# Hybrid decoder trunk on one core: the systems' products move behind the next pair's projections, and ScalarE takes copies out of PSUM

## The chip, the cores and the metric

The kernel runs on one core of one Trainium2 chip. The metric is the device time of one execution in microseconds (us). The engines of the core are TensorE (PE in the profile; PEld is its weight load), VectorE (DVE), ScalarE (ACT), GpSimd (POOL) and SyncE (SP, which issues nearly all DMAs here). PSUM is the memory that TensorE writes, SBUF the working memory.

## The reference, cut to what matters

One layer over 2048 tokens of width 1024. A combined projection `p = rms_norm(x) @ w_in` feeds five branches; each branch's output is projected up, weighted with a sigmoid gate, and the sum goes through `w_out`, a residual and a last norm. Three pieces of it concern the change:

```
# retention: rotate q and k, then chunks of 128 with a fixed decay
x1 * cos - x2 * sin,  x2 * cos + x1 * sin
scores = (q @ k.T) * seg;  y = scores @ v + (q * exp(cum)) @ prev_state
# RWKV-7: one state update per token
sa = state @ a_t
state = state * w_t + sa b_t^T + v_t k_t^T
y_t = state @ r_t
```

The kernel computes the RWKV recurrence in chunks of 64 tokens. For each head and chunk it forms a triangular system from products of decayed keys and "a" vectors, inverts it, and uses the inverse in a chain over the chunks.

## The kernel before, in words

The sequence is worked through in four blocks of 512 tokens. In each block the stages are: cross-attention (`mem`), preparation and solve for RWKV (`rwkv_first`), retention (`ret`), the RWKV chain (`rwkv`), the state-space branch, GLA, and the output product. Activations are kept transposed, 128 channels by 512 tokens to a tile.

A projection (`proj`, through `mm3`) is 24 matmuls of 128x128 by 128x512: 8 slices of the input, each in three parts, since values are split into a high and a low part. It accumulates in one of three PSUM tiles named `acc`; other products use three tiles `br` and two `y`. Weights come through a ring of four tiles `wt`, loaded by SP; in the first block they are loaded raw and split by ScalarE (`L378`) and GpSimd (`L379`). All matmuls but transposes are recorded at line L305, tensor-tensor operations of VectorE at L299, scalar-tensor-tensor ones at L302, and most activations at L296. Work tiles in SBUF are 42 tiles of one tag, `s`.

Gate and up-projection work of the previous branch waits in a queue (`self.fq`), in pieces: a gate piece is one projection, an up piece of the memory branch is 6 matmuls. `self.fill(n)` takes n pieces from it; `self.solve(n)` takes n steps from a second queue `self.dq`, which holds the 31 steps of the triangular solve.

`rwkv_prep` loops over four pairs of heads. For each pair: projection k, its squares, projection r, then `late()` of the pair before (with a piece of the queue ahead of it), the small products with `w2a2` (L1107, L1108), a chain of some twenty elementwise operations on VectorE, ScalarE and GpSimd that ends in the tiles `ars` and `kbs` (L1142 to L1146), their stores to DRAM (L1150), projection v, and then the systems' products (L1158): 32 matmuls of 64x64. Their masked result goes to `Ab` and, by four copies, to `dia` (L1165). `late` does the bonus term and the transposes of v, and stores both (L1173, L1179).

`rwkv_solve` prepares `X` and the 31 steps, each a multiplication (L1203) and a reduction (L1204) on VectorE; the later a step the larger. `ret` then runs `rope` for q and k (two projections each, four multiplications on VectorE that read both `acc` tiles from PSUM, two sums on GpSimd, eight stores at L695), `v_tok` (the values by token: 96 matmuls into four PSUM tiles, then four copies out at L714), and two pairs of heads. Each pair begins with a transposed k that VectorE scales (L764). `rwkv_sys`, which uses the solve (transposes L1219 and L1221, copies L1226), comes after `ret`.

Outside the very first stage a scheduler orders the instructions of each engine when the program is built, by its own estimate of their durations; the order in the program is the priority. On the chip every engine, and SP's queue of DMAs, runs through its list in that order.

Of the kernel before, what the change touches and what calls it, by code (L numbers as in the profile page):

```python
# [13 lines left out]
ALU = mybir.AluOpType  # L14
# [3 lines left out]
P = 128  # L18
# [20 lines left out]
def _groups():  # L39
# [3 lines left out]
    def add(name, c):  # L43
        g[name] = len(cols)
        cols.append(np.asarray(c, np.int64))

    def nat(name, key, n):
        for i in range(n):
            add(f"{name}{i}", _OFF[key] + 128 * i + np.arange(128))

    half = np.concatenate([64 * h + 2 * np.arange(32) for h in range(4)])
    for nm in ("q", "k"):
        add(f"ret_{nm}A", _OFF[f"ret_{nm}"] + half)
        add(f"ret_{nm}B", _OFF[f"ret_{nm}"] + half + 1)
    nat("ret_g", "ret_g", 4)
# [89 lines left out]
class K:  # L145
# [531 lines left out]
    def rope(self, nmq, sn, cs):  # L677

        nc = self.nc
        st = [self.s() for _ in range(2)]  # L680
        A = self.proj(f"ret_{nmq}A")
        B = self.proj(f"ret_{nmq}B")
        for i in range(2):
            t1, t2, o = self.s(), self.s(), self.s()
            if i == 0:
                self.tt(t1, A, cs, ALU.mult)
                self.tt(t2, B, sn, ALU.mult)
                nc.gpsimd.tensor_tensor(o, t1, t2, ALU.subtract)
            else:
                self.tt(t1, B, cs, ALU.mult)  # L690
                self.tt(t2, A, sn, ALU.mult)
                nc.gpsimd.tensor_tensor(o, t1, t2, ALU.add)
            for h in range(4):
                r = 64 * (h % 2) + 32 * i
                nc.sync.dma_start(st[h // 2][r:r + 32, :], o[32 * h:32 * h + 32, :])  # L695
        return st

    def v_tok(self, key):

        ps = [self.ps("acc") for _ in range(3)] + [self.ps("y")]  # L700
        for k in range(KT):
            (hi, lo), = self.load_w(("wv_" + key, k), 4)
            whi, wlo = (t.rearrange("p h d -> p (h d)") for t in (hi, lo))
            xhi, xlo = self.xh[k]
            for c in range(4):
                cs_ = slice(c * P, (c + 1) * P)
                self.mm(ps[c], xhi[:, cs_], whi, start=(k == 0), stop=False)
                self.mm(ps[c], xhi[:, cs_], wlo, start=False, stop=False)
                self.mm(ps[c], xlo[:, cs_], whi, start=False, stop=(k == KT - 1))
        vs = []  # L710
        for c in range(4):
            v = self.s()
            nc_copy = (self.nc.scalar.copy, self.nc.vector.tensor_copy)[c % 2]
            nc_copy(v, ps[c])  # L714
            vs.append(v)
        return vs

# [25 lines left out]
    def ret(self, sc):  # L743
        nc = self.nc
        sn, cs = self.tables
        q = self.rope("q", sn, cs)
        self.solve(K.FILL["solve"][0])
        k = self.rope("k", sn, cs)
        self.solve(K.FILL["solve"][1])
        V = self.v_tok("ret")  # L750
        self.solve(K.FILL["solve"][2])
        res = []
        for p in range(2):
            qh = self.s()
            self.tt(qh.rearrange("p (c t) -> p c t", t=P), q[p].rearrange("p (c t) -> p c t", t=P),
                    self.c["qd"][:, p * P:(p + 1) * P].unsqueeze(1).to_broadcast([P, 4, P]), ALU.mult)
            tp = self.ps("br")
            for c in range(4):
                self.tr(tp[:, c * P:(c + 1) * P], k[p][:, c * P:(c + 1) * P])
            kt = self.s()  # L760
            for j in range(2):
                h = 2 * p + j
                v4 = lambda t: t.rearrange("p (c h d) -> p c h d", h=2, d=64)[:, :, j, :]
                nc.vector.tensor_scalar(v4(kt), v4(tp), self.c["kd"][:, h:h + 1], None, ALU.mult)  # L764

            sp = self.ps("br")
            for c in range(4):
                cs_ = slice(c * P, (c + 1) * P)
                for j in range(2):
                    self.mm(sp[64 * j:64 * j + 64, cs_], kt[:, c * P + 64 * j:c * P + 64 * j + 64],  # L770
                            V[c][:, (2 * p + j) * P:(2 * p + j + 1) * P])
            S = self.states("Sret", self.S_ret, p, 4)
            for c in range(4):
                self.stt(S[c + 1], S[c], self.c["gC"][:, p:p + 1], sp[:, c * P:(c + 1) * P], ALU.mult, ALU.add)
            pts = []
            for j, sps in enumerate(self.scores(k[p], q[p])):
                pt = self.s()
                h = 2 * p + j
                self.tt(pt.rearrange("p (c t) -> p c t", t=P), sps.rearrange("p (c t) -> p c t", t=P),
                        self.c["dec"][:, h * P:(h + 1) * P].unsqueeze(1).to_broadcast([P, 4, P]), ALU.mult)  # L780
                pts.append(pt)
            ys = [self.ps("y") for _ in range(2)]
            self.solve(K.FILL["solve"][3])
            self.fill(K.FILL["ret"][0])
            for j in range(2):
                for c in range(4):
                    cs_ = slice(c * P, (c + 1) * P)
                    self.mm(ys[j][:, cs_], V[c][:, (2 * p + j) * P:(2 * p + j + 1) * P], pts[j][:, cs_],
                            start=(c == 0), stop=False)
            self.fill(K.FILL["ret"][1])  # L790
            for c in range(4):
                cs_ = slice(c * P, (c + 1) * P)
                for j in range(2):
                    r = slice(64 * j, 64 * j + 64)
                    self.mm(ys[j][:, cs_], S[c][r, :], qh[r, cs_], start=False, stop=(c == 3))
            res += self.finish_pair(sc, "ret", p, ys, self.cv["one"], K.FILL["ret"][2])
            self.solve(K.FILL["solve"][4])
        return res
# [283 lines left out]
    def rwkv_prep(self, wa, pairs):  # L1082
        nc = self.nc
        v3 = lambda t: t.rearrange("p (c t) -> p c t", t=64)
        am = self.c["am"]
        Ab = []
        gC = self.s((P, 4, 8), tag="gC", bufs=2)
        dia = self.s((P, 32, 32), tag="blk", bufs=3)
# [5 lines left out]
        late = None  # L1094
        for i, p in enumerate(pairs):
# [28 lines left out]
            rk = self.s()  # L1124
            self.stt(rk, r, self.p["r_k"][:, pc], kp, ALU.mult, ALU.mult)
            rk = self.parts(rk, self.pick(7))
# [3 lines left out]
            v = self.s()  # L1130
# [6 lines left out]
            ars, kbs = [], []  # L1137
# [13 lines left out]
                                      t.rearrange("p c a t -> p c (a t)"))  # L1151
            v = self.shift(8 + p)

            ap = self.ps("br")
            for c in range(8):
                for q in range(2):
                    rq = slice(64 * q, 64 * q + 64)
                    self.mm(ap[rq, c * 64:c * 64 + 64], kbs[c // 4][rq, c % 4, 1, :], ars[c // 4][rq, c % 4, 0, :])  # L1158
            ab = self.s((P, 8, 64))
            self.tt(ab, ap.rearrange("p (j t) -> p j t", t=64),  # L1160
                    am[:, 0:64].unsqueeze(1).to_broadcast([P, 8, 64]), ALU.mult)
            Ab.append(ab)
            for g in range(4):
                rg, b = slice(32 * g, 32 * g + 32), g % 2
                (nc.scalar.copy, nc.gpsimd.tensor_copy)[g % 2](  # L1165
                    dia[rg, :, i * 8:i * 8 + 8], ab[rg, :, 32 * b:32 * b + 32].rearrange("s j t -> s t j"))

            def late(p=p, rk=rk, v=v):
                bps = self.ps("br")
                self.msum(bps, self.bones_r, rk)  # L1170
                bv = self.s()
                self.tt(bv, bps, v, ALU.mult)
                nc.sync.dma_start(self.bvd[p], bv)  # L1173
                tp = self.ps("br")
                for c in range(4):
                    self.tr(tp[:, c * P:(c + 1) * P], v[:, c * P:(c + 1) * P])
                vt = self.s()
                nc.scalar.copy(vt, tp)
                nc.sync.dma_start(self.vtd[:, p, :].rearrange("(c r) d -> r c d", r=P),  # L1179
                                  vt.rearrange("p (c d) -> p c d", d=P))  # L1180

        self.fill(K.FILL["late"][3])
        late()
        return Ab, dia, gC

    def rwkv_solve(self, dia):

# [25 lines left out]
    def rwkv_sys(self, Ab, X):  # L1213

        nc = self.nc
        self.solve()
        self.fill(K.FILL["sys"][0])
        xa = self.s((P, 32, 32), tag="blk", bufs=3)
        nc.vector.transpose(xa, X.rearrange("p s c -> p c s"))  # L1219
# [3 lines left out]
        for i in range(4):  # L1223
            for g in range(4):
                r, b = slice(32 * g, 32 * g + 32), g % 2
# [131 lines left out]
    def rwkv_first(self, sc):  # L1357

        wa = self.shift(12)
        self.nc.scalar.activation(wa[0:64, :], wa[0:64, :], AF.Tanh)  # L1360
        Ab, dia, gC = self.rwkv_prep(wa, range(4))
        X, self.dq = self.rwkv_solve(dia)
        return Ab, X, gC

    def rwkv(self, sc):
# [300 lines left out]
```

## Time and profile before

| | us |
|---|---|
| median of 3 runs (3663.86 to 3673.31) | 3667.82 |
| the profiled execution, its own time | 3665.22 |
| its span, first to last instruction | 3663.4 |
| TensorE busy | 3444.2 |
| VectorE busy | 1992.8 |
| ScalarE busy | 983.5 |
| GpSimd busy | 917.4 |

The mean granted clock of TensorE is 0.966 of full. An idle time is given with what released it: `<-POOL s L1145` means that the engine waited for a GpSimd instruction of line 1145 that writes a tile `s`. A timeline merges like instructions; `x16` counts them.

### The profile page before, as it was taken

How to read it: one execution, taken by the hardware profiler on the slowest of the kernel's cores; microseconds unless marked ns; L12 is line 12 of the kernel's file. 1: busy time of each engine (PE TensorE's matmuls, PEld its weight loads, DVE VectorE, ACT ScalarE, POOL GpSimd, SP SyncE). 2: the span in 40 equal slices, each digit the busy share in tenths (PEclk: the TensorE clock that was granted, in tenths of full speed). 3: DMA queues.
4: the chain of work that ended last, by engine and by line, in shares of the span. 5: the costliest groups of instructions: out<-in, count | busy, mean ns of one | idle time of the engine just before them, and what ended most of it. 6: DMA issues, size and time to landing. Idle time of an engine off the chain costs nothing. (4 is left out here: it accounts for less than half of the span.)

```text
span 3663.4 us, 51984 instructions
## 1 busy us (share of the span) xinstructions
PE 3444.2 (94%) x20368; PEld 2766.4 (76%) x20368; DVE 1992.8 (54%) x3188; ACT 983.5 (27%) x1797; POOL 917.4 (25%) x919
## 2 busy tenths in 40 slices
PE   7878999998999899999999899999999989999998
PEld 6667777777777677888877677788887768778887
DVE  6685456635467645552356854554346664554243
ACT  5423224342442111312133121222123311131212
POOL 3655335555423110211103210021101311020110
PEclk9889899999999999999999999999999999999999
DMA  6566646676765444545565554445465645344555
GB/s 213 191 204 208 212 166 220 210 256 225 268 207 187 157 156 140 190 155 170 174 213 194 178 157 153 156 151 188 156 220 187 191 155 165 132 163 150 172 170 192
DMA packets 269541, 673.17 MB, mean 184 GB/s; under 512 B 27232, under 2 KB 81008, under 8 KB 269296
## 3 DMA queue, kind: packets, MB, share of 16 engines
q1 hardware_dynamic: 268864, 669.32, 54.8%
q8 instruction: 161, 2.64, 0.3%
q14 instruction: 84, 0.69, 0.1%
q10 hardware_dynamic: 432, 0.52, 0.0%
HBM read 503.54 MB, written 162.00 MB: 182 GB/s over the span
## 5 line engine op out<-in xcount | busy, mean ns | idle before, releaser
L305 PE MATMUL acc<-xhi,wt 128*128 128x512 f32 x5632 | 1832.3, 401 | 21.3 <-ACT s L296 9.5
L305 PEld LDWEIGHTS acc<-xhi,wt 128*128 128x128 f32 x5632 | 1076.6, 192 | 264.4 <-issue 13.3
L305 PE MATMUL acc<-xlo,wt 128*128 128x512 f32 x2816 | 1124.9, 399 | 2.5 <-DVE xlo L1542 1.8
L305 PE MATMUL acc<-s,wt 128*128 128x512 f32 (+1 forms) x2448 | 602.4, 396 | 30.5 <-ACT s L714 15.7
L305 PEld LDWEIGHTS acc<-xlo,wt 128*128 128x128 f32 x2816 | 541.7, 192 | 118.1 <-DVE xlo L1542 3.0
L305 PEld LDWEIGHTS acc<-s,wt 128*128 128x128 f32 x2448 | 459.0, 192 | 131.6 <-ACT s L714 17.0
L302 DVE SCALAR_TENSOR_TENSOR s<-s,acc 128x512 f32<-128x512 f32 x192 | 131.5, 685 | 668.5 <-PE acc L305 363.3
L379 POOL TENSOR_TENSOR wt<-wr,wt 128x512 fp32r<-128x512 f32 (+1 forms) x256 | 354.1, 1389 | 379.7 <-ACT wt L378 360.2
L302 DVE SCALAR_TENSOR_TENSOR s<-s,s 128x512 f32<-128x512 f32 (+1 forms) x458 | 368.1, 807 | 31.9 <-ACT s L296 19.8
L379 POOL TENSOR_TENSOR s<-s,s 128x512 fp32r<-128x512 f32 x120 | 159.9, 1341 | 858.7 <-ACT s L378 650.4
L296 ACT ACTIVATE s<-acc 128x512 f32<-128x512 f32 x232 | 136.4, 596 | 646.1 <-PE acc L305 633.5
L305 PE MATMUL br<-s,s 64*64 64x64 f32 (+6 forms) x2432 | 213.4, 284 | 75.0 <-POOL s L1145 33.6
L305 PEld LDWEIGHTS br<-s,s 64*64 64x64 f32 (+3 forms) x2432 | 164.7, 171 | 128.0 <-POOL s L1145 38.3
L378 ACT CAST wt<-wr 128x512 fp32r<-128x512 f32 (+1 forms) x256 | 155.4, 611 | 293.2 <-PE acc L305 102.5
L1406 POOL TENSOR_TENSOR mg<-mg,s 128x512 f32<-128x512 f32 x64 | 87.2, 1363 | 545.9 <-DVE s L302 545.9
L378 ACT CAST s<-s 128x512 fp32r<-128x512 f32 x182 | 112.7, 620 | 344.6 <-DVE s L302 328.2
L296 ACT ACTIVATE s<-s 128x512 f32<-128x512 f32 (+1 forms) x204 | 119.3, 611 | 287.2 <-DVE s L299 116.6
L299 DVE TENSOR_TENSOR s<-s 128x512 f32<-128x512 f32 (+1 forms) x167 | 162.4, 977 | 5.8
L305 PE MATMUL acc<-wt,xhi 128*128 128x512 f32 x384 | 123.2, 401 | 26.6 <-DMA wt<-kw 10.0
L305 PE MATMUL y<-s,s 128*64 128x64 f32 (+4 forms) x2112 | 136.8, 253 | 6.9 <-DVE s L299 4.4
L305 PEld LDWEIGHTS y<-s,s 128*64 128x64 f32 (+2 forms) x2112 | 112.2, 151 | 37.8 <-DVE s L299 10.9
L299 DVE TENSOR_TENSOR s<-s,s 128x512 f32<-128x512 f32 (+2 forms) x154 | 119.1, 798 | 37.6 <-ACT s L296 36.0
(218 smaller groups left out, 3208.7 us busy)
## 6 DMA issues: line engine op xcount, KB each, us to landing
wt<-kw SPq DMA_DIRECT2D x712, 512.0 KB, 3.3
kw<-wt SPq DMA_DIRECT2D x240, 512.0 KB, 3.1
wr<-in_wg_dram SPq DMA_DIRECT2D x176, 256.0 KB, 3.8
s<-in_xT_dram SPq DMA_DIRECT2D x88, 256.0 KB, 5.0
ard<-s SPq DMA_DIRECT2D x32, 256.0 KB, 2.2
kbd<-s SPq DMA_DIRECT2D x32, 256.0 KB, 2.5
s<-kbd SPq DMA_DIRECT2D x32, 256.0 KB, 4.1
s<-ard SPq DMA_DIRECT2D x32, 256.0 KB, 4.8
```

The lines of the kernel that those rows point to most:

```text
L296: self.nc.scalar.activation(out, in_, f, bias=bias, scale=scale, **kw)
L299: self.nc.vector.tensor_tensor(out, a, b, op)
L302: self.nc.vector.scalar_tensor_tensor(out, a, s, b, op0, op1)
L305: i = self.nc.tensor.matmul(out, lhsT=lhsT, rhs=rhs, start=start, stop=stop)
L378: self.nc.scalar.copy(hi, src)
L379: (eng or self.nc.gpsimd).tensor_tensor(lo, src, hi.bitcast(F32), ALU.subtract)
L1406: (eng or self.pick({"ret": 0, "rwkv": 1, "ssd": 2, "gla": 3}[key])).tensor_tensor(merged[d], merged[d], t, ALU.add)
```

## The change

In `rope`, the two projections A and B are each copied by ScalarE from PSUM to a work tile; the multiplications read the copies. In `v_tok`, all four copies of retention's values are ScalarE's; for GLA they still alternate between ScalarE and VectorE. In `rwkv_prep`, the systems' products with their mask and copies move into `late`, which runs after the next pair's projections k and r. The last pair's `late`, the queue piece ahead of it and the setting up of the solve leave `rwkv_first`: they run after the rotation of q in `ret`, as the first entry of the solve's queue.

```diff
     def rope(self, nmq, sn, cs):
...
-        A = self.proj(f"ret_{nmq}A")
-        B = self.proj(f"ret_{nmq}B")
+        A, B = self.s(), self.s()
+        for t, c in ((A, "A"), (B, "B")):
+            nc.scalar.copy(t, self.proj(f"ret_{nmq}{c}"))
...
     def v_tok(self, key):
...
-            nc_copy = (self.nc.scalar.copy, self.nc.vector.tensor_copy)[c % 2]
-            nc_copy(v, ps[c])
+            if c % 2 and key != "ret":
+                self.nc.vector.tensor_copy(v, ps[c])
+            else:
+                self.nc.scalar.copy(v, ps[c])
...
     def ret(self, sc):
         q = self.rope("q", sn, cs)
+        self.fill(K.FILL["late"][3])
         self.solve(K.FILL["solve"][0])
...
     def rwkv_prep(self, wa, pairs):
...
             v = self.shift(8 + p)
-            ap = self.ps("br")
-            for c in range(8):
-                for q in range(2):
-                    rq = slice(64 * q, 64 * q + 64)
-                    self.mm(ap[rq, c * 64:c * 64 + 64], kbs[c // 4][rq, c % 4, 1, :], ars[c // 4][rq, c % 4, 0, :])
-            ab = self.s((P, 8, 64))
...
-            def late(p=p, rk=rk, v=v):
+            def late(i=i, p=p, rk=rk, v=v, ars=ars, kbs=kbs):
+
+                ap = self.ps("br")
+                for c in range(8):
+                    for q in range(2):
+                        rq = slice(64 * q, 64 * q + 64)
+                        self.mm(ap[rq, c * 64:c * 64 + 64], kbs[c // 4][rq, c % 4, 1, :], ars[c // 4][rq, c % 4, 0, :])
+                ab = self.s((P, 8, 64))
...
                 bps = self.ps("br")
                 self.msum(bps, self.bones_r, rk)
...
-        self.fill(K.FILL["late"][3])
-        late()
-        return Ab, dia, gC
+        return Ab, dia, gC, late
...
     def rwkv_sys(self, Ab, X):
         self.solve()
+        X, = X
...
     def rwkv_first(self, sc):
...
-        Ab, dia, gC = self.rwkv_prep(wa, range(4))
-        X, self.dq = self.rwkv_solve(dia)
+        Ab, dia, gC, late = self.rwkv_prep(wa, range(4))
+        X = []
+
+        def begin():
+            late()
+            x, self.dq = self.rwkv_solve(dia)
+            X.append(x)
+
+        self.dq = [begin]
         return Ab, X, gC
```

## Rows read from the trace of the kernel before

**Rows 1.** The page, part 1: busy us (share) x instructions of each engine.

```profile
PE 3444.2 (94%) x20368; PEld 2766.4 (76%) x20368; DVE 1992.8 (54%) x3188; ACT 983.5 (27%) x1797; POOL 917.4 (25%) x919
```

**Rows 2.** Waits of TensorE, whole span: us in total, times, longest us.

```profile
PE br L305 <- POOL s L1145: 33.6, 12, 4.6
PE br L305 <- DVE s L302: 22.0, 4, 6.1
...
PE acc L305 <- DVE s L299: 16.0, 7, 4.6
PE acc L305 <- ACT s L714: 15.7, 3, 5.7
PE acc L305 <- DMA wt<-kw: 10.0, 7, 2.3
```

**Rows 3.** Waits of TensorE from 220 to 345 us, the first block's retention.

```profile
PE acc L305 <- POOL wt L379: 8.3, 3, 4.8
```

**Rows 4.** Timeline of TensorE, fourth block: start us, us, what, idle before.

```profile
2879.27 1.54 PE L305 MATMUL br<-s,w2a 64*128 64x256 f32 x8
...
2894.02 0.61 PE L305 MATMUL acc<-xhi,wt 128*128 128x512 f32 x2
2897.06 0.68 PE L305 MATMUL br<-s,s 64*64 64x64 f32 x16 [2.43 <-POOL s L1145]
...
2899.31 1.22 PE L305 MATMUL acc<-xhi,wt 128*128 128x512 f32 x2
...
2923.57 0.68 PE L305 MATMUL br<-s,s 64*64 64x64 f32 x16 [2.56 <-POOL s L1145]
```

**Rows 5.** Windows: 16 stretches at half clock; us, PE busy, PEclk, DMA.

```profile
2898.10:2901.50 3.40, 3.32 (x22) 0.50 0.85 224
...
sum 78.60, PE 69.85; mean PE 4.37
```

**Rows 6.** Timeline of VectorE, fourth block, retention with the solve.

```profile
2927.63 1.25 DVE L1191 STREAM_TRANSPOSE blk<-blk 128x1024 f32<-128x1024 f32 x1 [0.66 <-POOL blk L1165]
...
2938.55 0.68 DVE L299 TENSOR_TENSOR s<-acc,s 128x512 f32<-128x512 f32 x1
...
2945.36 0.68 DVE L299 TENSOR_TENSOR s<-acc,s 128x512 f32<-128x512 f32 x1
...
2952.19 0.68 DVE L299 TENSOR_TENSOR s<-acc,s 128x512 f32<-128x512 f32 x1
...
2978.66 1.21 DVE L1221 STREAM_TRANSPOSE blk<-blk 128x1024 f32<-128x1024 f32 x1
2979.78 0.66 DVE L714 COPY s<-acc 128x512 f32<-128x512 f32 x1
...
2981.88 0.86 DVE L764 TENSOR_SCALAR s<-br,cst 128x256 f32<-128x256 f32 x2
```

**Rows 7.** Timeline of TensorE, fourth block, after V's matmuls.

```profile
2983.76 2.93 PE L305 MATMUL acc<-s,wt 128*128 128x512 f32 x6 [5.71 <-ACT s L714]
```

**Rows 8.** Timeline of ScalarE, the same stretch.

```profile
2978.77 4.46 ACT L1226 COPY s<-blk 32x256 f32<-32x256 f32 x7 [50.65 <-DVE blk L1219]
```

**Rows 9.** Timeline of SP's queue, fourth block: start us, us, issue.

```profile
2922.64 0.37 SPq L1150 DMA_DIRECT2D ard<-s  x1
...
2955.12 2.41 SPq L695 DMA_DIRECT2D s<-s  x4
```

**Rows 10.** Groups by line and form: busy us, mean ns | idle before.

```profile
L296 ACT ACTIVATE s<-acc 128x512 f32<-128x512 f32 x232 | 136.4, 596 | 646.1 <-PE acc L305 633.5 <-issue 12.6
L299 DVE TENSOR_TENSOR s<-s,s 128x512 f32<-128x512 f32 x116 | 98.0, 870 | 37.6 <-ACT s L296 36.0
L299 DVE TENSOR_TENSOR s<-acc,s 128x512 f32<-128x512 f32 x48 | 31.4, 682 | 19.1 <-PE acc L305 19.1
```

**Rows 11.** Chain that ended last, 3000 to 3020 us: start us, us, what.

```profile
3005.31 11.11 PE acc L305 x48
```

**Rows 12.** The page, part 6: DMA issues, KB each, us to landing.

```profile
wt<-kw SPq DMA_DIRECT2D x712, 512.0 KB, 3.3
```

More of the change, by code (lines that the diff above doesn't have):

```diff
@@ L1152, in rwkv_prep @@
             v = self.shift(8 + p)
-            ap = self.ps("br")
-            for c in range(8):
-                for q in range(2):
-                    rq = slice(64 * q, 64 * q + 64)
-                    self.mm(ap[rq, c * 64:c * 64 + 64], kbs[c // 4][rq, c % 4, 1, :], ars[c // 4][rq, c % 4, 0, :])
-            ab = self.s((P, 8, 64))
[L1160 to L1166, printed above, removed]
-            def late(p=p, rk=rk, v=v):
+            def late(i=i, p=p, rk=rk, v=v, ars=ars, kbs=kbs):
[5 more added lines that the diff above has]
+                ab = self.s((P, 8, 64))
+                self.tt(ab, ap.rearrange("p (j t) -> p j t", t=64),
+                        am[:, 0:64].unsqueeze(1).to_broadcast([P, 8, 64]), ALU.mult)
+                Ab.append(ab)
+                for g in range(4):
+                    rg, b = slice(32 * g, 32 * g + 32), g % 2
+                    (nc.scalar.copy, nc.gpsimd.tensor_copy)[g % 2](
+                        dia[rg, :, i * 8:i * 8 + 8], ab[rg, :, 32 * b:32 * b + 32].rearrange("s j t -> s t j"))
                 bps = self.ps("br")
```

## The prediction

> **What bounds the kernel now.** The page comes first. TensorE is busy for 94% of the span, no other engine for more than 54% [rows 1]. So the time is TensorE's work plus its idle time, and an edit is worth what it takes from that idle time, or from the work done at a low clock. The view of waits, for TensorE alone, then shows where the idle time lies [rows 2]. The two largest entries, 33.6 + 22.0 = 55.6 us in 16 waits, stand in front of one thing: the systems' products of rwkv_prep (L1158), four in each of the four blocks of tokens. Four further entries belong to the stretch after them, the retention stage: 16.0 us for accumulators that VectorE's rotation still reads, 15.7 us for ScalarE's copies of V, 10.0 us for weights not landed [rows 2], and in the first block 8.3 us for weights that GpSimd splits [rows 3]. That makes 50.0 us.
>
> The timeline of TensorE shows what one product wait looks like [rows 4]. The small products L1107 end at 2880.81 (2879.27 + 1.54). TensorE goes on with projections until 2894.63, then waits 2.43 us. The products start at 2897.06, 16.25 us after L1107. In between it had about 13.8 us of work, since the scheduler took the chain on VectorE and GpSimd for shorter than it is. The two projection matmuls ahead of the wait took 0.61 us, the two after it 1.22 us. The windows give the reason: after each of the 16 waits stands a stretch with granted clock 0.50, the lower of the two levels (1.2 GHz). They add up to 78.6 us, 69.85 of them busy [rows 5]. What the engine did before each was to stand idle.
>
> For the retention stage I read three engines in one stretch. VectorE runs the 62-step solve from 2927.63 to 2979.78 without a pause, and the rotation's multiplications stand between its steps [rows 6]. TensorE waits 5.71 us at 2983.76 for ScalarE's V copy [rows 7]. ScalarE had stood 50.65 us in front of L1226, which needs the end of the solve, with the V copies queued behind [rows 8].
>
> **Part 1, the products behind the next pair's projections.** Work stays the same; order changes. Two projections of 24 matmuls take 11.1 us [rows 11], 5.55 each. Between L1107 and the products TensorE will have the pair's v projection, the next pair's k and r projections, and a unit of the queue: a gate (5.55) three times of four, an up product (6 matmuls, 1.4) once, since the queue begins with gate, gate, up, gate. That is 16.65 + 5.55 = 22.2 us, or 18.0 us. The chain needs 16.25 us, so the wait goes: -55.6 us. The first block is slower, with waits near 6 us [rows 2], so its chain is some 3 us longer; there the pair with the short unit still waits. I leave +4 us for that and its clock. The half-clock time goes with the waits. It costs at most half of its busy time, 34.9 us, and at least nothing; I take 30, because projection matmuls, most of that time, took exactly double.
> The Trainium skill (TensorE: Matmul & The Clock Gate, section Terms) prices such time as throttled time times one minus the clock ratio: 39.3 us as an estimate from that page, by which the sum would be 9 us lower. The trace bears the halving out, but 8.75 us of the stretch were idle.
>
> The four stores of a pair (ard, kbd) keep their place on SP's queue, as do bvd and vtd of the first three pairs; the last pair's follow q's eight stores, whose inputs are ready before the solve starts. Nothing waits for them before the chain stage.
>
> **Part 2, the last pair and the solve behind the rotation of q.** The order is now v, q's two projections, a gate, the products: 22.2 us after L1107 instead of 16.25. The solve starts 4.06 us after the products' start, as now (2923.57 to 2927.63) [rows 4, 6]. What is queued behind the solve on VectorE is the rotation of k and retention's first pair.
>
> **Part 3, ScalarE's copies.** 16 copies of A and B and 8 of V at 0.596 us [rows 10] are 14.3 us on an engine busy for 27%, hidden in its 50.65 us pause [rows 8] and its like; if that cover went, 3.6 us a block. An accumulator is then free 0.6 us after its last matmul instead of after VectorE's turn, so 16.0 us go, and 15.7 us go if the V copies stand ahead of L1226. They should: now the solve's last transpose (2978.66) and the first V copy (2979.78) are neighbours [rows 6], so any later start of the solve turns their order round. SP's stores of the rotated k hold the weight loads up [rows 9]; they wait for GpSimd and so for VectorE. With the solve started later VectorE is less far behind at that point, and I let the 10.0 go, and the 8.3 of the first block, where ScalarE's weight casts stood behind L1226 too. In all -50.0 us. Six or seven of those waits were long, and after one the six matmuls took 2.93 us instead of 1.4 [rows 7, 11]: another -9.
> 32 multiplications now read two SBUF tiles: 0.870 us instead of 0.682 on the mean [rows 10]. Sixteen, those of k, fall into the solve. The Trainium skill (GPSIMD Engine Reference, 1. Specifications) says that GpSimd shares its SBUF interface with VectorE and contends with instructions that have two SBUF inputs; that speaks against this edit, the two rows agree with it, and by it the sum would be 16 x 0.19 = 3 us higher.
>
> **What is late next.** VectorE. The scheduler lined the multiplications at 2938.55, 2945.36 and 2952.19 up with the ends of successive projections [rows 6]. TensorE needs 5.55 us for each, VectorE took 6.8: it runs 1.25 times slower than the order supposes, so it falls behind as long as it is full. TensorE next needs VectorE in retention's first pair: the scaled transpose of k (L764), for which V's copies had been the cover [rows 6, 7]. In the new order the products take some 2.4 us (2897.06 to 2899.31 and a little), k's rotation 11.1 and V's 96 matmuls 22.2: V ends 35.7 us after the products' start, 31.7 after the solve's. VectorE needs 31.7 x 1.25 = 39.6 us for what stands before L764. So a new wait of 8 us a block, 32 us, and 1.7 us of clock each, 7 us: +39. Bounds: nothing, if other work stands in front of it; and 17.7 us a block if L764 follows the whole solve. The solve without eight multiplications is 52.15 - 5.4 = 46.7 us, with four 49.4; it ends 53.4 us after the products' start, 17.7 after V.
>
> **Sum.** The profiled execution took 3665.2 us. 3665.2 - 55.6 - 30 + 4 - 50 - 9 + 39 = 3563.6. The median of the runs is 2.6 us above that execution: **3566 us**.
>
> **Rivals.**
> No late VectorE (12%): the queue's units cover L764. For it: a gate is 5.55 us and one is queued there. Against it: the order supposes no wait, so it has no reason to put more than a short unit in front. -39: 3527 us.
> ScalarE stays behind the solve (16%): L1226 is still queued ahead of V's copies, now all four on that engine. Then TensorE waits from V's end to the end of the solve and its copies, 17.7 + 4.46 = 22.2 us a block [rows 8]; 89 in place of 32: 3623 us. Against it: the solve starts later.
> The change doesn't do what it says (6%): the scheduler goes by readiness, and puts the products where they stand now if weights or accumulators of the next projections aren't free. Then -55.6, -30 and +4 stay out: 3648 us. Against it: TensorE ran into k's projection ahead of the products already now [rows 4].
> Slower (6%): the weight ring. TensorE no longer rests while SP stands in front of the ard and kbd stores [rows 9]. A load lands 3.3 us after its issue [rows 12] and its slot is due three tiles, 8.2 us, later, which leaves 4.9. The stores come about as much later than the order supposes as the products do now, 2.4 us, so this is hidden. The rival decides if loads land 10 us after issue or later: each pair then waits 6 us + 1.9 of clock, 16 x 7.9 = 126 us: 3692 us.
>
> **How the numbers follow.** The forecast has 55%, with a range of its own from 3545 to 3590. With two of the rivals, 3527 and 3623, the range from 3525 to 3625 holds 83%. 5% are left for mixtures that end near 3668. A measurement of this kernel tells no change from 0.3%, 11 us. Faster: 55 + 12 + 16 + 6, less 1 for scatter: 0.88; same 0.05; slower 0.07.
>
> **What would show it.** Right: the entries GpSimd L1145 and VectorE L302 ahead of 64x64 products are gone; no half clock between pairs; products stand 18 to 22 us after L1107; ScalarE's V copies stand ahead of L1226; TensorE waits some 8 us a block for L764. Wrong: the products still wait; V copies behind L1226; waits for weights in rwkv_prep. The prediction fails most easily in the new order of retention's first pair, which the trace of before doesn't show.

## The result, and the profile after

The changed kernel takes 3613.65 us (median of 4 runs, 3611.5 to 3618.59) against 3665.84 us (4 runs): a ratio of 0.9858, 95% interval 0.9837 to 0.9879. It is faster by 52 us; forecast were some 100. 3613.65 lies inside the stated range, 3525 to 3625, but outside the forecast's own, 3545 to 3590. The profiled execution has a span of 3616.7 us, 46.7 less than before; its mean granted clock is 0.967. Of the 46.7 us, 15.6 are busy time of TensorE (3444.2 before [rows 1]) and 31.1 idle time:

```profile
PE 3428.6 (95%) x20368; PEld 2760.3 (76%) x20368; DVE 1993.1 (55%) x3180; ACT 997.8 (28%) x1821; POOL 914.8 (25%) x919
```

The view of waits, TensorE alone, whole span (engine, what it waited for: us in total, times, longest):

```profile
PE br L305 <- DVE s L768: 26.9, 5, 6.2
PE br L305 <- DVE s L299: 25.0, 12, 5.5
PE acc L305 <- ACT wt L378: 11.5, 3, 7.2
...
PE acc L305 <- DMA wt<-kw: 9.2, 6, 2.4
...
PE acc L305 <- POOL wt L379: 7.5, 5, 4.2
...
PE br L305 <- POOL s L1149: 6.3, 2, 3.1
```

Gone are the waits for GpSimd (L1145, now L1149) and VectorE in front of the systems' products, all but 6.3 us and 1.4 in the first block, and those for the rotation and for V's copies [rows 2]. The 6.3 us stand at the first pair of blocks 3 and 4. There 14 of the 32 products stand ahead of one of the four projections that were to cover them, and the chain was not done; in the fourth block:

```profile
2804.08 1.08 PE L305 MATMUL br<-s,s 64*64 64x64 f32 x14 [3.14 <-POOL s L1149]
```

To weigh the first two lines, these are the same entries before (L764 is now L768):

```profile
PE acc L305 <- POOL wt L379: 8.9, 4, 4.8
PE acc L305 <- ACT wt L378: 7.0, 1, 7.0
PE br L305 <- DVE s L299: 6.7, 8, 4.1
PE br L305 <- DVE s L764: 4.7, 2, 4.3
```

So two waits grew where large ones went: for a VectorE result of L299 by 18.3 us, and for the scaled transpose of k by 22.2.

**The first of them** stands in the preparation. TensorE in the fourth block, around the products of the second pair and of the third (start us, us; x32 counts instructions; in brackets the idle time in front and what ended it):

```profile
2839.06 1.15 PE L305 MATMUL br<-s,s 64*64 64x64 f32 x32
...
2841.24 1.54 PE L305 MATMUL br<-s,w2a 64*128 64x256 f32 x8
...
2859.82 1.52 PE L305 MATMUL acc<-s,wt 128*128 128x512 f32 x6
2861.28 1.15 PE L305 MATMUL br<-s,s 64*64 64x64 f32 x32
...
2866.46 1.73 PE L305 MATMUL br<-s,w2a 64*128 64x256 f32 x8 [2.93 <-DVE s L299]
```

The systems' products (64x64) start without a wait, 18.5 us after the end of the small products of their pair (2842.78 to 2861.28; before, 16.25 for this pair). But the next small products (`w2a`) now wait 2.93 us. VectorE at that time:

```profile
2864.45 0.75 DVE L302 SCALAR_TENSOR_TENSOR s<-u,par,s 128x512 f32<-128x512 f32 x1 [2.58 <-ACT s L296]
2865.12 0.68 DVE L302 SCALAR_TENSOR_TENSOR mg<-s,acc 128x512 f32<-128x512 f32 x1
2865.72 0.69 DVE L299 TENSOR_TENSOR s<-br,cst 128x512 f32<-128x512 f32 x1
```

The mask multiplication `s<-br,cst`, which reads the systems' products and so frees their `br` tile, ends at 2866.41, and the small products start at 2866.46. There are three `br` tiles; `late` now takes all three (products, bonus, transposes), and the small products follow it. The mask stands behind the shift of the next r, whose projection was issued just before the 6 matmuls of an up product. VectorE was itself idle for 2.58 us in front of that shift, until ScalarE had handed it over, while the products had ended at 2862.43; whether the mask, put ahead of the shift in VectorE's list, would take the wait away was not tried. Where a whole gate was the piece (2839.06) the wait is absent, but for 3.39 us in block 1 and 0.85 in block 2. Over the four blocks the waits for the mask are 18.5 us, 14.3 of them behind the short piece.

**The second** stands in retention's first pair. TensorE, VectorE and ScalarE in the fourth block:

```profile
2931.54 1.64 PE L305 MATMUL acc<-s,wt 128*128 128x512 f32 x6
...
2939.84 5.31 PE L305 MATMUL br<-s,s 128*64 128x128 f32 x32 [6.20 <-DVE s L768]
```
```profile
2935.98 1.68 DVE L299 TENSOR_TENSOR blk<-blk,blk 128x900 f32<-128x900 f32 x1
2937.70 1.09 DVE L1206 TENSOR_REDUCE blk<-blk 128x30 f32<-128x900 f32 x1
...
2939.30 0.87 DVE L768 TENSOR_SCALAR s<-br,cst 128x256 f32<-128x256 f32 x2
```
```profile
2929.39 1.90 ACT L717 COPY s<-acc 128x512 f32<-128x512 f32 x3 [22.75 <-PE acc L305]
...
2948.57 5.39 ACT L1229 COPY s<-blk 32x256 f32<-32x256 f32 x8 [16.55 <-DVE blk L1222]
```

V's copies stand ahead of the solve's copies (L1229), as forecast. VectorE goes through the solve up to its last step but one (128x900) before it comes to L768, and TensorE waits 6.20 us.

The granted clock is read from the windows. The sums over all stretches at 0.50 in the preparation (8 of them) and in retention (9, the last one shown), then the last stretch and the sum of a list for retention before (8):

```profile
sum 40.94, PE 36.09; mean PE 4.51
...
2936.50:2946.74 10.24, 6.90 (x36) 0.50 0.00 0
sum 64.84, PE 49.81; mean PE 5.53
```
```profile
2983.40:2986.81 3.41, 3.04 (x7) 0.50 0.00 0
sum 37.55, PE 32.53; mean PE 4.07
```

The list before begins with the stretch at 218.60 (6.83 us, 5.29 of them busy), which stands behind the last product wait of the first block and is among the 16 of [rows 5] too; without it retention had 30.7 us, 27.24 busy. The preparation before had, beside those 16, one stretch that stands behind no product wait (95.72, 6.83 us, 6.17 busy); its counterpart is among the 8 after. So in the preparation the half clock fell from 85.4 to 40.9 us, and in retention it rose from 30.7 to 64.8. At each first pair's wait for L768 stand 10.24 us at 0.50, in which the 32 matmuls of the states and the scores take 5.31 us; after the 5.71 us for V before it was 3.41 us [rows 7].

### The profile page after: what moved, and what is told of

Its sections match the earlier page's. It is cut to its first block, busy times and chain, and to the rows that moved or that the text cites. A ratio compares the mean times of both kernels' runs of the same rounds, so it can differ in the third digit from the quotient of the medians.

```text
span 3616.7 us, 52010 instructions
## 1 busy us (share of the span) xinstructions
PE 3428.6 (95%) x20368; PEld 2760.3 (76%) x20368; DVE 1993.1 (55%) x3180; ACT 997.8 (28%) x1821; POOL 914.8 (25%) x919
## 3 DMA queue, kind: packets, MB, share of 16 engines
q1 hardware_dynamic: 268864, 669.32, 55.6%
## 4 chain that ended last, share of the span: by engine, by line
PE 55%; DVE 10%; issue 1%; DMA 1%; ACT 1%; POOL 0%; SPq 0%; DVEq 0%; POOLq 0%; ACTq 0%
PE acc L305 44%; PE br L305 6%; PE y L305 4%; DVE s L302 4%; DVE s L299 2%; DVE blk L299 2%; DVE blk L1206 1%; PE br L317 1%; DMA s<-ard 1%; ACT s L296 1%; DVE s L339 0%; DVE s L329 0%; DMA s<-in_xT_dram 0%; ACT blk L1171 0%; DMA s<-kmd 0%
## 5 line engine op out<-in xcount | busy, mean ns | idle before, releaser
L379 POOL TENSOR_TENSOR wt<-wr,wt 128x512 fp32r<-128x512 f32 (+1 forms) x256 | 354.8, 1391 | 380.1 <-ACT wt L378 369.3
L379 POOL TENSOR_TENSOR s<-s,s 128x512 fp32r<-128x512 f32 x120 | 159.7, 1339 | 816.6 <-ACT s L378 672.3
L378 ACT CAST wt<-wr 128x512 fp32r<-128x512 f32 (+1 forms) x256 | 155.2, 611 | 268.3 <-PE acc L305 89.6
L378 ACT CAST s<-s 128x512 fp32r<-128x512 f32 x182 | 112.8, 620 | 341.4 <-DVE s L302 316.6
L299 DVE TENSOR_TENSOR s<-s,s 128x512 f32<-128x512 f32 (+2 forms) x186 | 144.2, 803 | 44.5 <-ACT s L296 42.2
L299 DVE TENSOR_TENSOR s<-s 128x512 f32<-128x512 f32 (+1 forms) x167 | 163.0, 980 | 5.8
```

Of the source, the lines that this page charges most:

```text
L299: self.nc.vector.tensor_tensor(out, a, b, op)
L378: self.nc.scalar.copy(hi, src)
L379: (eng or self.nc.gpsimd).tensor_tensor(lo, src, hi.bitcast(F32), ALU.subtract)
```

## The experiments

The theory to test: the moved products bring the gain; the shortfall is the two new waits with their clock, and waits for weights that didn't go. Rivals are named at each run.

**1. Only the copies; 2. only the moves.** The first has the hunks in `rope` and `v_tok`, the second all the others.

> The kernel before with ScalarE's copies of the rotation's operands and of all of retention's values, and nothing moved. Theory (the moved products bring the gain, and the copies give back what they take away by making VectorE's scaled transpose of k late): the 16.0 us of waits for accumulators held by the rotation go, some of the 15.7 us for V's copies too, and waits for the scaled transpose with half-clock time behind them take their place; 3665.8 before, 3645 to 3672 here, a ratio of 0.995 to 1.002. Rival (the copies bring most of the gain of 52 us, the moved products little): 3615 to 3635, a ratio below 0.992.

Measured: 3683.43 us, ratio 1.0051 (1.0037 to 1.0066), slower than before and outside both ranges. The copies alone lose 20 us. In the profile the accumulator waits for the rotation are gone, but:

```profile
PE acc L305 <- DMA wt<-kw: 20.3, 11, 2.7
PE acc L305 <- ACT s L717: 18.6, 3, 6.6
```
```profile
sum 85.37, PE 68.73; mean PE 5.73
```

Weights come later (10.0 before), V's copies still stand behind the solve's, and retention has 85.4 us at half clock instead of 37.6 (both lists with the stretch at 218): 36.2 us more busy time there, half of which, 18.1 us, would be loss. By the page, TensorE's busy time grew by 12.5 us (3444.2 to 3456.7) and the span by 17.4, so the clock is most of the difference and not all of it. The wait for L768 that I had expected did not appear.

> The changed kernel with the moved products, last pair and solve, but the rotation reads PSUM and the copies of V alternate, as before. Theory (the moved products bring the gain): the 56 us of product waits are replaced by some 27 us of others, half-clock time in the preparation falls by some 41 us of stretch, 20 us of time; the accumulator waits of the rotation stay or grow a little: 3610 to 3632, a ratio of 0.985 to 0.991. Rival (the copies bring it): 3640 to 3660, a ratio of 0.993 to 0.999.

Measured: 3616.77 us, 0.9873 (0.9853 to 0.9892). The moves bring 47 of the 52 us; the interval overlaps that of the whole change. Part of the rotation's waits stays, and waits for V's copies on VectorE stand beside them (the profiled execution took 3601.86 us, 15 less than the median):

```profile
PE acc L305 <- DVE s L299: 12.1, 4, 4.0
...
PE acc L305 <- DVE s L714: 9.0, 4, 3.5
```

**3. The transposed k scaled by ScalarE.**

```diff
-                nc.vector.tensor_scalar(v4(kt), v4(tp), self.c["kd"][:, h:h + 1], None, ALU.mult)
+                self.act(v4(kt), v4(tp), AF.Copy, scale=self.c["kd"][:, h:h + 1])
```

> The changed kernel, but ScalarE scales the transposed k instead of VectorE (L768). Theory (VectorE behind the solve, alone, makes the wait of 26.9 us and the half clock after it): the waits go, the half-clock stretches after them (four of about 10.2 us, half of it lost) too: 3613.7 less 23 to 27 of waits less about 20 of clock, 3567 to 3585. Rival (the wait only moves on to the next results of VectorE, the masked scores and the states, which stand behind the same solve): the entry of L768 is gone and others of VectorE (L299, L302) grow by as much, 3605 to 3617.

Measured: 3612.27 us, 0.9865 (0.9846 to 0.9884), no change. My theory of a single late instruction falls. TensorE, fourth block:

```profile
2937.96 2.25 PE L305 MATMUL br<-s,s 128*64 128x128 f32 x32
...
2948.46 3.62 PE L305 MATMUL y<-s,s 128*128 128x128 f32 x16 [7.13 <-DVE s L299]
```

The 32 matmuls come earlier and at full clock, and then TensorE waits 7.13 us for the masked scores, also VectorE's and behind the same solve. Waits of this kind (`y <- DVE s L299`) are 32.6 us in all, 4.9 in the changed kernel.

**4. One more piece ahead of the third pair's products.** `"late": (1, 1, 2, 1)` in place of `(1, 1, 1, 1)`.

> The changed kernel with two pieces of the queue instead of one ahead of the third pair's small products, so that a full projection follows the short up product there. Theory (the small products wait because the mask multiplication, which frees their PSUM tile, has only the short piece as cover): the waits of 18.5 us for the mask fall by the 15 or so that stand at the third pair, with some of the half clock behind them: 3592 to 3605. Rival (the tile is short wherever the piece stands, since the mask stands behind VectorE's other work, or the piece taken from later leaves a hole there): the waits move, 3608 to 3625.

Measured: 3654.32 us, 0.9969 (0.9957 to 0.9981), 41 us slower than the changed kernel, worse than either range. The wait entry of the mask fell from 25.0 to 11.8 us, as forecast, and was paid for elsewhere:

```profile
PE br L305 <- DVE s L768: 40.0, 8, 8.3
PE acc L305 <- ACT s L296: 26.0, 10, 6.2
```

All later pieces of the queue changed places, gates for up products. Run 6 holds them in place.

**5. Pieces ahead of the late product in retention.**

```diff
+            if p == 0:
+                self.fill(2)
             sp = self.ps("br")
...
-            self.fill(K.FILL["ret"][1])
+            self.fill(K.FILL["ret"][1] - 2 * (p == 0))
```

> The changed kernel, but in retention's first pair two pieces of the queue (a short one and a whole gate) stand ahead of the product that needs the scaled transpose of k (L768), and two fewer behind it; VectorE's work is the same. Theory (VectorE is late by a few us and TensorE merely lacks cover; scaling on ScalarE only moved the wait on to the masked scores): the L768 waits of 22.7 us at four first pairs go, the masked scores have the next short piece and arrive in time, the half clock behind goes: 3613.7 - 22.7 - about 20 = 3570, 3565 to 3590. Rival (VectorE's solve is the bound of the whole stretch, so a wait of the same size comes up further back, at the masked scores, the states or the systems' stage): 3605 to 3620.

Measured: 3608.34 us, 0.9845 (0.9826 to 0.9865). The rival is right but for a few us: L768 falls to 8.3 us, and 23.2 us stand at the masked scores.

```profile
PE y L305 <- DVE s L299: 23.2, 16, 4.8
```

Runs 3 and 5 say the same: not one instruction is late, all that VectorE does behind the solve is.

**6. The same pieces in the same order, the short one earlier.** `"late": (1, 2, 1, 0)`.

> The changed kernel with the same pieces of the queue in the same order, but a gate follows the short up product already ahead of the second pair, and none is left for the last pair; behind the preparation the queue stands as before. Theory (the third pair's small products wait for the mask because their only cover is the short piece; with one piece more in all, the loss came from the shifted queue in retention): the waits for the mask at the third pair go (some 15 us with block 1's), those of L768 stay within 3 us of 26.9, the last pair's products may wait 1 us a block: 3590 to 3606. Rival (the mask's tile is short wherever pieces stand): 3610 to 3620.

Measured: 3602.28 us, 0.9821 (0.9804 to 0.9838), 11 us under the changed kernel. The mask's entry falls from 25.0 to 9.8 us, L768 stays at 25.8. So the short piece as only cover made most of that wait (block 1's 3.39 us stays), and with the queue held in place run 4's loss is gone. That the shift made the loss is argued from this, not shown.

**7. The small products ahead of the systems' products.** `late()` stands behind the two `w2a2` loops instead of before them.

> The changed kernel with the small products of the next pair ahead of the systems' products of the last one, so that they don't wait for the PSUM tile that the mask has to free. Theory (the tile, not the time at which VectorE reaches the mask, makes the wait of 18.5 us): those waits go, and none of over 1 us stands at the small products; 3613.7 - 18.5 - about 6 of half clock = 3589, 3583 to 3600. Rival (the third tile is then missed by the bonus and transposes behind the mask): the wait moves to the bones product or to L317, 3608 to 3620.

Measured: 3628.26 us, 0.9896 (0.9879 to 0.9914), slower than the changed kernel and beyond the rival's range. Its mechanism holds: in blocks 2 to 4 a wait of 2.91 us for the mask stands at the next product into a `br` tile, the bones product; products wait 15.6 us for the chain again (GpSimd, L1150), weights 19.7 us.

**8. The stores of the rotated k issued by ScalarE.**

```diff
-                nc.sync.dma_start(st[h // 2][r:r + 32, :], o[32 * h:32 * h + 32, :])
+                (nc.scalar if nmq == "k" else nc.sync).dma_start(st[h // 2][r:r + 32, :], ...)
```

> The changed kernel with the eight stores of the rotated k issued by ScalarE instead of SP. Theory (the weight loads of V stand on SP's queue behind k's stores, and so behind VectorE): the waits for weights in retention, 9.0 us with block 1's, go, and the half clock behind some of them: 3600 to 3608. Rival (the loads are late for another reason, the ring's slots): they stay within 2 us, 3610 to 3618. In either case the wait for L768 grows by what TensorE arrives earlier, so the time itself may not move; then the entries decide.

Measured: 3614.52 us, 0.9852 (0.9833 to 0.9872), no change.

```profile
PE br L305 <- DVE s L768: 38.9, 5, 10.4
...
PE acc L305 <- DMA wt<-kw: 4.4, 3, 2.6
```

Half of the waits for weights go (9.2 us in the changed kernel): those loads did stand behind k's stores on SP's queue. The wait for L768 is 12.0 us longer, and the time is what it was: with VectorE late, the weights cost nothing that the runs can tell.

**9. The solve's last five steps behind the first pair's masked scores.** `order` puts an instruction behind another in an engine's list. The counts let 26 steps be called before the first pair.

```diff
-"solve": (4, 4, 6, 4, 6)
+"solve": (8, 8, 11, 2, 3)
...
+            if self.behind is not None and not self.strict:
+                self.order(i, self.behind)      # i: a step's multiplication
...
+            if p == 0:
+                self.behind = i                 # i: the last masked score
```

> The changed kernel, but the last five steps of the solve (n = 27 to 31, some 13 us of VectorE) may stand only behind the masked scores of retention's first pair in VectorE's list; the work is the same, and the systems' stage needs the solve only some 75 us later. Theory (VectorE is late at L768, the states and the masked scores because the order puts the solve's large steps in front of them, by too short an estimate): the L768 waits of 22.7 us go without coming up at the scores, with half the half-clock stretches behind them (four of about 10 us): 3613.7 - 22.7 - 15 to 20 = 3571 to 3576, range 3565 to 3595. Rival (VectorE is short of time in the whole of retention, or the clock falls there for another reason): the waits move behind the first pair, 3605 to 3617.

Measured: 3587.11 us, 0.9783 (0.9770 to 0.9797), 26 us under the changed kernel. TensorE and VectorE, fourth block:

```profile
2911.84 2.95 PE L305 MATMUL br<-s,s 128*64 128x128 f32 x32
...
2915.89 2.05 PE L305 MATMUL y<-s,s 128*128 128x128 f32 x16
```
```profile
2911.01 0.88 DVE L768 TENSOR_SCALAR s<-br,cst 128x256 f32<-128x256 f32 x2 [3.16 <-PE br L317]
...
2915.15 1.28 DVE L783 TENSOR_TENSOR s<-br,cst 128x512 f32<-128x512 f32 x2
2916.35 1.45 DVE L1206 TENSOR_TENSOR blk<-blk,blk 128x729 f32<-128x729 f32 x1
```
```profile
sum 23.88, PE 21.34; mean PE 4.27
```

Now VectorE waits for TensorE. The first pairs wait neither for L768 nor for the scores (the 6.2 us left under L768 are one wait in block 1's second pair), and retention's half clock falls from 64.8 to 23.9 us. The time is within the range of the theory, 11 us above its point: the entries for weights and their casts (L378, L379) are together 7 us longer than in the changed kernel.

**10. Steps and pieces together; 11. the same without ScalarE's copies; 12. run 10 with run 8's stores.**

> The same with the queue's pieces 1, 2, 1, 0 ahead of the pairs' products, which alone gave 11 us. Theory: the two add up, since they stand at different places: 3560 to 3585, faster than either alone. Rival: they stand in each other's way, since the last pair's products come without a piece and the solve then starts earlier against TensorE's work: not more than 5 us under the steps alone.

Measured: 3573.93 us, 0.9752 (0.9738 to 0.9765). They add up: 13 us under run 9.

> As the run before, but without ScalarE's copies: the rotation reads PSUM, and V's copies alternate. It asks what the copies are worth once VectorE isn't late: with VectorE late they were worth 3 us. Theory (the copies take 20 to 30 us of accumulator and V waits away and were only masked by VectorE): this kernel is 10 to 30 us slower than the run before. Rival (the copies are worth nothing either way, since weights and VectorE's slower two-operand multiplications give it back): within 6 us of the run before.

Measured: 3561.36 us, 0.9720 (0.9704 to 0.9736), 13 us faster than run 10. Neither expectation: without the copies the kernel is better. It is the best version of the study, 104 us under the kernel before.

> The kernel with the copies, the steps behind and the pieces 1, 2, 1, 0 (3573.9 us), with the eight stores of the rotated k issued by ScalarE. Without the copies that kernel took 3561.4 us, and its waits for weights were 5.4 us against 15.0. Theory (the copies cost because k's stores, and the weight loads behind them on SP's queue, come later; with VectorE late this was hidden behind L768): the waits for weights fall to 5 to 9 us and the time to 3560 to 3567. Rival (the 12 us lie in other stages, whose order and clock shift with any edit): the waits for weights fall, the time stays between 3569 and 3578.

Measured: 3572.75 us, 0.9751 (0.9733 to 0.9770), as run 10 and as the rival had it. The waits for weights fall from 15.0 to 2.4 us, and L768 comes back: 4.4 us in run 10, here 18.3 in 4 waits.

So taking the waits for weights away alone does not give the 13 us between runs 10 and 11 back; as in run 8, VectorE takes them over, and this does not clear the weights. Between the profiled executions of runs 10 and 11 (spans of 3580.1 and 3569.6 us) the largest differences are in the waits for weights (15.0 to 5.4 us) and for ScalarE's casts of them (12.5 to 8.0), against L768 (4.4 to 8.0) and the rotation (0.5 to 4.8). Which of them makes the 13 us stays open.

## Why the prediction was right or wrong

By the terms of the sum, in the profiled executions. The gain of clock is taken as half of the busy time at 0.50, of the same stages before and after; the product and L768 terms are taken from the entries above and [rows 2].

| term | predicted | measured |
|---|---|---|
| product waits, with residue | -51.6 | -55.6 + 6.3 + 0.9 + 18.3 = -30.1 |
| half clock in the preparation | -30 | (36.09 - 69.85 - 6.17) / 2 = -20.0 |
| waits in retention | -50 | -16.0 - 15.7 - 0.8 - 1.4 + 4.5 = -29.4 |
| half clock in retention | -9 + 7 = -2 | (49.81 - 27.24) / 2 = +11.3 |
| new wait for VectorE (L768) | +32 | +22.2 |
| sum | -101.6 | -46.0 (span: -46.7) |

That the sum meets the span is partly chance: its waits make -37.3 and its clock -8.7, where idle time fell by 31.1 and busy time by 15.6. So other waits grew by some 6 us, and some 7 us of busy time went that the sum doesn't hold.

The direction held: the waits went where I had said, and the late VectorE came. But the gain is half of the forecast, and that it lies in the range is luck: the part above 3590 was there for the rival at 3623, whose cause, V's copies behind the solve, did not come. The sum failed at four places.

- **"Work stays the same; order changes."** The waits in front of the products went, mostly at the 18 to 22 us after the small products that I had worked out. What is left of them is not where the +4 had put it: the chain's 16.25 us were read off one pair, and the first pair of the fourth block had needed 21.6 before (2815.92 + 1.13 to 2838.65) and needed 21.7 after (2782.36 to 2804.08). The step that failed is that nothing else would wait: I followed the products' inputs and not the tile that they write. The tile is needed by the small products, which the move made their neighbours. Run 6 shows the place, and the missing cover as cause: 15 us less of that wait, 11 us of time.
- **The half clock of the preparation.** It went with the waits, and came again with the new ones: of the eight stretches left (40.9 us), five (23.9) stand at the waits for the mask, as the last, 2868.23 to 2871.64, behind the wait at 2866.46; two (13.65) stand at the 6.3 us of product waits that are left.
- **"VectorE is less far behind at that point, and I let the 10.0 go, and the 8.3 of the first block."** That was a hope. Weights still took 9.2 us and the first block's casts and splits rose by 3.1 in all. Run 8 shows why half of the weights' waits are there (k's stores, and so VectorE), and no cost of them as long as VectorE was late behind them.
- **1.7 us of clock for each late wait.** The stretch behind L768 is 10.24 us with 6.90 busy: 3.45 us each. I had priced it by what followed V's wait, six matmuls; here 32 small ones follow.

The new wait itself was forecast at 8 us a block and measured at 5.97 to 6.20 in blocks 2 to 4, 4.31 in the first. VectorE took 43.6 us from the solve's start (2895.70) to L768 (2939.30), where I had 39.6 (with 1.25 for what is 6.8 / 5.55 = 1.23; with that, 38.8); V ended 35.5 us after the solve's start, not 31.7, with 2.96 us of waits for weights in it that I had let go. Both sides were some 4 us short, so the 8 us between them came out right by luck; some 2 us of other work of TensorE made it a wait of 6.

Of the rivals, V's copies behind the solve came true where only the copies were made (run 1), not in the change. That the scheduler leaves the products where they were came true for 14 of the 32 products at two first pairs and nowhere else. The weight ring did not: 9.2 us of waits for weights in all. The Trainium skill's rule on the shared interface (GPSIMD Engine Reference, 1. Specifications) had been priced at 3 us for k's multiplications; those ran at 0.64 us in the fourth block, with GpSimd idle at the time, so that price did not come due there.

What the copies are worth I had wrong: I gave them -50 and -9. Alone they cost 20 us (run 1), on top of the moves they bring 3, which is not more than the runs scatter, and with VectorE in time they cost 13 (runs 10, 11). The waits that they remove are real [rows 2]; what they cost is shown for run 1 alone, as later weights and time at half clock in retention, and is open for run 10.

## What to carry to other kernels

When a wait is taken from the bound engine, ask of every moved instruction which tile it takes and who needs that tile next, and look for the engine that was late behind the wait: it gets the time. A late engine isn't helped by covering or moving one of its instructions (runs 3 and 5), nor by removing a wait ahead of it (run 8); take work that nobody needs yet out of its way, as run 9 did. Change a queue of filler work without shifting what comes after it, or the shift can hide the effect, as it seems to have done in run 4 beside run 6.

## What the runs showed of the hardware

A wait's price in clock isn't set by its length alone: 5.71 us in front of 128x512 projections were followed by 3.41 us at 0.50, 3.04 of them busy [rows 7]; a shorter wait, 4.31 us in front of 32 small matmuls, stands at a stretch of 10.24 us, 7.05 of them busy. The first block of the changed kernel:

```profile
273.88 5.31 PE L305 MATMUL br<-s,s 128*64 128x128 f32 x32 [4.31 <-DVE s L768]
```
```profile
270.69:280.93 10.24, 7.05 (x36) 0.50 0.57 188
```

In blocks 2 to 4 the stretch is 10.24 us long too, at waits of 5.97 to 6.20 us. What follows the wait differs between the two cases, and so may where it falls; which of these decides was not tried.

In these runs a step of VectorE that begins while a sum of GpSimd runs takes longer; one that has begun before the sum does not, and then the sum is the longer one. In the changed kernel's fourth block, steps of the solve (two SBUF inputs) and GpSimd's sums of the rotation:

```profile
2909.77 0.76 DVE L299 TENSOR_TENSOR blk<-blk,blk 128x324 f32<-128x324 f32 x1
...
2911.09 1.28 DVE L299 TENSOR_TENSOR blk<-blk,blk 128x361 f32<-128x361 f32 x1
...
2912.96 0.92 DVE L299 TENSOR_TENSOR blk<-blk,blk 128x400 f32<-128x400 f32 x1
...
2915.60 1.65 DVE L299 TENSOR_TENSOR blk<-blk,blk 128x441 f32<-128x441 f32 x1
...
2917.93 1.04 DVE L299 TENSOR_TENSOR blk<-blk,blk 128x484 f32<-128x484 f32 x1
```
```profile
2909.93 1.75 POOL L689 TENSOR_TENSOR s<-s,s 128x512 f32<-128x512 f32 x1 [13.25 <-DVE s L299]
2915.16 1.29 POOL L693 TENSOR_TENSOR s<-s,s 128x512 f32<-128x512 f32 x1 [3.48 <-DVE s L299]
```

The 361 and 441 columns began inside a sum and took 1.28 and 1.65 us; the longer 400 and 484 columns, alone, took 0.92 and 1.04. The 324 columns began 0.16 us ahead of the sum, ran beside it and took 0.76, as they do alone in run 1 (0.77 in blocks 2 to 4); that sum took 1.75 us, the next one, which began beside no such step, 1.29. The same two forms without a sum are in other runs: 361 columns 0.84 us in run 6, 441 columns 0.98 in the kernel before, each in blocks 2 to 4.
